# Attention of four head pairs as one list of items, SSM rows stored in two parts, and the last branch's rows loaded earlier

## The chip, the core and the metric

The kernel runs on one core of a Trainium2 chip. TensorE (PE in the profile; its weight loads are PEld) multiplies, VectorE (DVE), ScalarE (ACT) and GpSimd (POOL) work on tiles, and SyncE (SP) issues the transfers. The metric is the device time of one execution in microseconds (us).

## What is computed

One layer of a hybrid encoder, for a prompt of 1024 tokens and 32 sample tokens with a cache of 512 past positions, model width 1024, all in fp32. Cut to what matters here:

```python
z = einsum('btd,de->bte', h, w_in)                  # h: modulated RMSNorm of x
u, zs, q, k, v, za, qi, ki, wi, gm = split(z)
ys = gelu(ssm_scan(u, ...))                         # branch A, width 512
ys = ys * sigmoid(ys @ w_glu + b_glu) * silu(zs)
score = einsum('bth,bths->bts', wi, relu(qi . ki))  # indexer, 8 heads
idx = top_k(score, 256)                             # per query, among causal keys
ya = attend(q, k[idx], v[idx]) * silu(za)           # branch B, 8 heads of 64
merged = sigmoid(g_s) * (ys @ w_ps) + sigmoid(g_a) * (ya @ w_pa)
y = rms_norm(x + gate * (merged @ w_o), g_final)
```

Keys, values, indexer keys and the final SSM states are outputs too.

## The kernel before

Every fp32 product is three matmuls: an operand is split in a high part, rounded to TensorE's fp32r format, and a low part, the remainder, and `mm3` adds high x high, weight high x low and weight low x high (lines 245 to 247). `split` (L53) makes the parts: a cast (L55 on ScalarE, L57 on another engine) and a subtraction (L58). Activations are kept with channels on partitions and 1056 tokens (1024 and 32) on the free axis, in three column blocks of 352, chosen by `ns(n)`.

On TensorE, VectorE and ScalarE the order of the program is the order in which the code is written. GpSimd's and SyncE's instructions are placed by a scheduler. Each engine runs its queue in order.

**The filler stream.** The products with `w_in` that a later stage needs are jobs of the stream `Z` (class `Stream`, L551). A job (K1, V1, Q1, and m0 to m7) yields a step after each `mm3` of one column block and one k: 24 steps for a `w_in` job of 8 k, 12 for an m job of 4. `Z.run(us)` takes steps worth that time, at 0.483 us each, `Z.until(name)` takes all up to a job's end, `Z.upto(name)` allows jobs up to that one, and `Z.after(us, f)` calls `f` after that many us of steps. A step that isn't there (all allowed jobs are used up) ends `run` and drops its credit.

**The stages,** as they lie in the trace of before: GLU (266 to 304 us) ends in `ysD`, the SSM branch's rows in DRAM. The indexer's scores follow, then the selection (420 to 570): 31 iterations search each query's threshold bit by bit, ScalarE counting (L1549) and VectorE counting (L1551), and VectorE updating the keys (L1621, L1628, L1614). K, V and Q of pair 0 are made under it: their splits run on VectorE (casts) and GpSimd (subtractions, L58 and L1348). Marks of the selected keys follow.

**Attention** runs over four head pairs (p = 0 to 3; 632 to 900 us). `attend(p, ...)` (L1387) has a list of items: for each head e of the pair eight row blocks of 128 queries (`Rows`), and one `Sample` item for the sample tokens. An item has five parts: scores (L1363), maxima with the mask (L1369, VectorE), exponentials (L1376, ScalarE), normalization (L1383 or L1385), transposes with split (L1446, L1448, L1449) and the product with V (`out`, L1465 its low half). They are taken as a pipeline: in round k the scores of item k, the output of item k − 3, the transposes of item k − 2 and the exponentials of item k, with filler between them. `attend` runs three rounds more with no new item, and then the caller takes the rest of Q of the next pair (`Z.until`) and splits V of the next pair (`values`, L1347 and L1348). K of a head is read from its tile into a shifted one by DMA (`khead`, `kd`). In pairs 0 to 2 the filler is K, V and Q of the next pair; in pair 3 it is m0 to m7.

**The SSM branch's products** (`psjob`, m0 to m7, `ys @ w_ps`) need `ys` in parts: `ps_branch` loads 12 blocks of 128x352 in four transfers' worth of buffers at the start of pair 3 and splits them on ScalarE and VectorE, four rounds in a row (`extra`). The m jobs also load gate rows (`tgl`) into buffers that they share (`stg`).

**The last branch** (`branch`, `ya @ w_pa`) starts after m7: it loads pairs 0 to 2's rows of `ya` from `yaD` (L1725) through the two `stg` buffers, splits each (1056 columns, L55 and L58) and runs 8 jobs of 12 `mm3`. Pair 3's parts (`b3H`, `b3L`) are made by the attention itself. Then come the output product and the final norm (930 to 1073).

## Time and profile before

| | us |
|---|---|
| median of 3 runs | 1079.08 |
| lowest and highest | 1078.77, 1080.61 |
| the profiled execution | 1074.72 |
| its span | 1072.9 |
| busy in it: TensorE, VectorE, ScalarE, GpSimd | 1000.9, 765.6, 537.1, 246.9 |

The profiled execution is one run with its own time, 0.4% below the median of the others; 1.8 us of it lie outside the span. Times in the rows below count from the span's start. The mean granted TensorE clock over the span is 0.978 of full speed; the column PEclk of a stretch gives the clock there. An idle time in brackets behind an instruction is that of its engine just before it, and the arrow names what ended last there. Some matmul records can be missing, so counts of matmuls in a stretch are a few per cent rough.

### The profile page before, as it was taken

Reading aid. Unit: us, or ns where it says so; the run is one execution under the profiler, and the core shown is the slowest. Engines: PE = TensorE matmul, PEld = TensorE weight load, DVE = VectorE, ACT = ScalarE, POOL = GpSimd, SP = SyncE. Lnnn points to the kernel's source line nnn. Section 1 sums busy time; section 2 is a strip of 40 time slices with the busy share of each in tenths; the row PEclk is TensorE's granted clock in tenths of the full one; section 3 lists DMA queues with packets and bytes.
Section 4 is the critical chain, followed back from the end, with each engine's and each line's share of the span. In section 5 each row is a group of like instructions: output and inputs, shape, how many; then the busy total and the mean of one; then the engine's idle time right before and its main releaser. Section 6 shows DMA issues by size and latency. Waiting matters only on the chain.

```text
span 1072.9 us, 17009 instructions
## 1 busy us (share of the span) xinstructions
PE 1000.9 (93%) x6130; PEld 926.7 (86%) x6130; DVE 765.6 (71%) x1757; ACT 537.1 (50%) x1145; POOL 246.9 (23%) x465
## 2 busy tenths in 40 slices
...
GB/s 349 218 43 120 108 81 93 79 107 200 160 157 102 59 40 39 71 69 92 80 100 80 121 102 60 121 59 78 64 51 100 130 63 173 172 170 138 112 75 59
DMA packets 114321, 115.24 MB, mean 107 GB/s; under 512 B 13121, under 2 KB 90901, under 8 KB 114237
## 3 DMA queue, kind: packets, MB, share of 16 engines
...
HBM read 79.29 MB, written 30.08 MB: 102 GB/s over the span
## 4 chain that ended last, share of the span: by engine, by line
PE 51%; ACT 9%; DVE 8%; issue 4%; DMA 1%; POOL 0%; POOLq 0%; ACTq 0%; DVEq 0%
PE pz L245 7%; PE pz L247 6%; PE pz L246 6%; ACT junkb L1549 6%; PE pss L1363 3%; PE pt L1446 3%; PE psm L1874 3%; PE psm L1876 2%; PE psm L1875 2%; PE pss L247 2%; PE pss L245 2%; PE pss L246 2%; DVE junk L1551 2%; PE pspo L1465 2%; PE pspo L1463 2%
## 5 line engine op out<-in xcount | busy, mean ns | idle before, releaser
L245 PE MATMUL pz<-hH,wh 128*128 128x352 f32 (+1 forms) x824 | 280.1, 340 | 6.8 <-DVE zt L669 4.3
L246 PE MATMUL pz<-hL,wh 128*128 128x352 f32 (+1 forms) x824 | 269.1, 327 | 0.8 <-DVE hL L58 0.2
L247 PE MATMUL pz<-hH,wl 128*128 128x352 f32 (+1 forms) x824 | 268.4, 326 | 0.0
L238 POOL TENSOR_TENSOR wl<-raw,wh 128x256 fp32r<-128x256 f32 (+1 forms) x184 | 130.5, 736 | 169.9 <-ACT wh L233 155.6
L245 PEld LDWEIGHTS pz<-hH,wh 128*128 128x128 f32 (+1 forms) x824 | 155.9, 189 | 11.8 <-DVE zt L669 4.9
L246 PEld LDWEIGHTS pz<-hL,wh 128*128 128x128 f32 (+1 forms) x824 | 156.0, 189 | 4.1 <-DVE hL L58 2.0
L247 PEld LDWEIGHTS pz<-hH,wl 128*128 128x128 f32 (+1 forms) x824 | 155.7, 189 | 0.4
L1549 ACT ACTIVATE junkb<-sco,thr 128x896 bf16<-128x896 f32 (+3 forms) x128 | 103.6, 809 | 27.9 <-DVE thr L1628 20.0
L1551 DVE TENSOR_SCALAR_CACHE_REDUCE junk<-sco,thr 128x1024 bf16<-128x1024 f32 (+2 forms) x96 | 96.9, 1010 | 2.3
L245 PE MATMUL pss<-hH,wh 128*128 128x352 f32 x256 | 84.5, 330 | 7.8 <-ACT tg L680 5.2
L247 PE MATMUL pss<-hH,wl 128*128 128x352 f32 x256 | 84.1, 328 | 1.2 <-POOL wl L238 1.2
L246 PE MATMUL pss<-hL,wh 128*128 128x352 f32 x256 | 83.8, 327 | 0.0
L237 POOL CAST wh<-raw 128x256 fp32r<-128x256 f32 x88 | 34.8, 434 | 166.5 <-PE pz L246 143.2
L1376 ACT ACTIVATE Sm<-Sm,mx 128x128 f32<-128x128 f32 (+8 forms) x68 | 52.6, 774 | 13.5 <-DVE mx L1369 13.4
L1449 DVE TENSOR_TENSOR PL<-pt,PH 128x512 fp32r<-128x512 f32 (+2 forms) x96 | 50.6, 552 | 11.3 <-ACT PH L1448 10.1
L245 PEld LDWEIGHTS pss<-hH,wh 128*128 128x128 f32 x256 | 49.1, 192 | 10.4 <-POOL wh L237 5.2
L1448 ACT CAST PH<-pt 128x512 fp32r<-128x512 f32 (+2 forms) x96 | 43.2, 481 | 27.4 <-PE pt L1446 24.8
L1207 DVE SCALAR_TENSOR_TENSOR sco<-rl,wi,sco 128x384 f32<-128x384 f32 (+6 forms) x49 | 47.3, 977 | 11.7 <-ACT rl L1202 10.1
L1202 ACT ACTIVATE rl<-pss 128x384 f32<-128x384 f32 (+6 forms) x56 | 40.9, 738 | 28.3 <-PE pss L1200 20.3
L233 ACT CAST wh<-raw 128x1024 fp32r<-128x1024 f32 (+2 forms) x43 | 36.1, 839 | 32.7 <-PE pz L246 21.0
L1876 PE MATMUL psm<-o,mL 128*128 128x512 f32 (+1 forms) x136 | 51.7, 382 | 0.0
L1875 PE MATMUL psm<-o,mH 128*128 128x512 f32 (+1 forms) x136 | 51.6, 381 | 0.0
...
## 6 DMA issues: line engine op xcount, KB each, us to landing
...
```

Source lines behind the costliest of these rows:

```text
L238: leng.tensor_sub(wl[:, c], raw[:, c], f32(wh[:, c]))
L245: te.matmul(ps, wh, xh, start=first, stop=False)
L246: te.matmul(ps, wh, xl, start=False, stop=False)
L247: te.matmul(ps, wl, xh, start=False, stop=last)
L1207: ve.scalar_tensor_tensor(sco[i][:m, :nk], rl[:m, :nk], w, sco[i][:m, :nk], op0=ALU.mult, op1=ALU.add)
L1376: se.activation(P, P, AF.Exp, scale=-1.0, bias=self.mx, accum_out=self.rs)
L1448: se.copy(PH[:, b0:b1_, oc], src)
L1449: ve.tensor_sub(PL[:, b0:b1_, oc], src, f32(PH[:, b0:b1_, oc]))
L1549: se.activation(junkb[:m, :nk], x[:m], AF.Sign, bias=t, accum_out=cnt[:m, k:k + 1])
L1551: ve.tensor_scalar(junk[:m, :nk], x[:m], t, None, op0=ALU.is_lt, op1=ALU.add, accum_out=cnt[:m, k:k + 1])
L1875: te.matmul(ps, mh, wl, start=False, stop=False)
L1876: te.matmul(ps, ml, wh, start=False, stop=last)
```

## The change

- **One list.** `attention(p, X)` only returns a pair's items. One loop runs over the items of all four pairs, so the last outputs of one pair stand in the rounds of the next pair's first scores. Filler is set per pair and head (`FA`, us per item, with `FF` per row block): 2.0 and 1.3 in pairs 0 and 1, 2.4 and 1.6 in pair 2, 1.5 in pair 3, where it was 1 (1.4 in pair 3). Q of the next pair is allowed from head 1 on. V is a tile per head; head 0's is split three rounds ahead of the pair's end, head 1's after the last output.
- **K** goes to DRAM once (`kd`) and is read back from there per head. The subtractions of pair 0's K and V run on VectorE (`heng_v`).
- **SSM rows in two parts.** GLU casts and subtracts its result per block of 352 columns on ScalarE and GpSimd and stores both parts (24 transfers of 128x352 instead of 4 of 128x1056). When Q3 ends, `switch` issues 24 direct loads of those parts, into the place of the activations' low part; no split is left. The m jobs start behind them, still under pair 2.
- **The last branch's rows** are loaded right after the last attention item, before the rest of m0 to m7, into buffers of their own (the place of the transposed scores and of the output weights), and split at 4, 5 and 6 us of the steps that follow.
- **Stream.** Where no step is available, `run` advances the delayed calls (`tick`).

```diff
@@ -35,7 +35,7 @@
-FA = ((1, 0.08), (1, 0.08), (1, 0.08), (1.4, 0.08))
+FA, FF, SW, SA, SB = ((2.0, 1.3), (2.0, 1.3), (2.4, 1.6), (1.5, 1.5)), 0.08, 1.2, 4.0, 1.0
@@ -616,19 +616,21 @@
...
-                for t in self.later:
-                    t[0] -= 1
-                for t in [t for t in self.later if t[0] <= 0]:
-                    self.later.remove(t)
-                    t[1]()
+                self.tick()
                 return True
+
+        def tick(self):
+            for t in self.later:
+                t[0] -= 1
+            for t in [t for t in self.later if t[0] <= 0]:
+                self.later.remove(t)
+                t[1]()
         def run(self, us):
             self.credit += us / self.STEP
             while self.credit >= 1:
                 if not self.step():
-                    self.credit = 0.0
-                    return
+                    self.tick()
                 self.credit -= 1
...
@@ -1061,7 +1063,7 @@
...
-    ysD = [dram.tile([128, NT], F32, name=f"ysD{q}") for q in range(4)]
+    ysD = [[dram.tile([128, NT], F32, name=f"ys{h}D{q}") for q in range(4)] for h in "HL"]
...
@@ -1093,8 +1095,10 @@
...
             ve.scalar_tensor_tensor(z2[:, c], th, 1.0, z2[:, c], op0=ALU.add, op1=ALU.mult)
-        sp.dma_start(ysD[q], z2)
...
+            yo = [gp.tile([128, G3], F32R, name=f"yo{h}", bufs=3) for h in range(2)]
+            split(yo[0], yo[1], z2[:, c], se, ge)
+            for h in range(2):
+                sp.dma_start(ysD[h][q][:, c], f32(yo[h]))
...
@@ -1254,10 +1258,10 @@
...
             for hf_ in range(2):
-                sp.dma_start(kd[64 * hf_:64 * hf_ + 64], X.kf[64 * e:64 * e + 64, c])
+                sp.dma_start(kd[64 * hf_:64 * hf_ + 64], X.kd[64 * e:64 * e + 64, c])
             def parts():
-                split(kH[:, c], kL[:, c], kd, ve, ge)
+                split(kH[:, c], kL[:, c], kd, ve, leng)
...
@@ -1309,6 +1313,9 @@
...
         def kside(self):
+            self.kd = dram.tile([128, T], F32, name=f"kd{self.p}")
+            sp.dma_start(self.kd, self.kf[:, 0:T])
+
...
@@ -1338,16 +1346,16 @@
...
-                khead(self, self.want.pop(0), KA, done)
-
-        def values(self):
-            V2 = self.V2 = ap_.tile([128, 8, 2, 128], F32R, name="V2", bufs=1)
-            for e in range(2):
-                vsrc = self.vt[:, 0:8, 64 * e:64 * e + 64]
-                ve.tensor_copy(V2[:, :, e, 0:64], vsrc)
-                ge.tensor_sub(V2[:, :, e, 64:128], vsrc, f32(V2[:, :, e, 0:64]))
-            self.cvt = ap_.tile([128, 4, 128], F32, name="cvt", bufs=1)
-            sp.dma_start(self.cvt, cv[:, :, self.cs])
+                khead(self, self.want.pop(0), self.heng_v, KA, done)
+
+        def values(self, e):
+            V = self.V2[e] = ap_.tile([128, 8, 128], F32R, name=f"V{e}", bufs=1)
+            vsrc = self.vt[:, 0:8, 64 * e:64 * e + 64]
+            ve.tensor_copy(V[:, :, 0:64], vsrc)
+            self.heng_v.tensor_sub(V[:, :, 64:128], vsrc, f32(V[:, :, 0:64]))
+            if e:
+                self.cvt = ap_.tile([128, 4, 128], F32, name="cvt", bufs=1)
+                sp.dma_start(self.cvt, cv[:, :, self.cs])
...
@@ -1384,22 +1392,32 @@
...
-    def attend(p, X, fills, half, last_s, extra=None):
-        kall, V2, vts, cvt = X.kall, X.V2, X.vts, X.cvt
-        qsm = X.qsm.rearrange("p e q -> p (e q)")
-        ya = at2.tile([128, NT], F32, name="ya", bufs=1)
+    def attention(p, X):
+
+        Y = {}
+
+        def begin():
+            if p < 3:
+                Y[0] = stg.tile([128, NT], F32, name="ya", tag="stg")
+                sp.dma_start(Y[0], zaD[p])
+            else:
+                Y[0] = f32(ap_.tile([128, T], F32R, name="qs1", bufs=2))
+                Y[1] = at2.tile([128, TS], F32, name="ys", bufs=1)
+                sp.dma_start(Y[0], zaD[p][:, 0:T])
+                sp.dma_start(Y[1], zaD[p][:, T:NT])
+
...
@@ -1480,39 +1498,7 @@
...
-        fa_, fb_ = fills
-        q = []
-        for k, it in enumerate(items + [None] * 3):
-            f = fa_ + fb_ * (it.i + 1 if it else 5)
-            if it:
...
-        if p < 3:
-            sp.dma_start(yaD[p], ya)
+        return items, begin, lambda: sp.dma_start(yaD[p], Y[0])
...
@@ -1556,7 +1542,8 @@
-        Z.after(1.0, X.values)
+        Z.after(1.0, lambda: X.values(0))
+        Z.after(2.0, lambda: X.values(1))
@@ -1565,31 +1552,16 @@
...
     def ps_branch():
-        bH, bL = ({(q, n): fb.tile([128, G3], F32R, name=f"b{h}{q}{n}") for q in range(4) for n in range(3)}
-                  for h in range(2))
-        src = {}
-
...
-        PB.extend((bH, bL))
-        for t in range(3):
-            load(t)
-        for b, c in ((0, 4), (4, 6), (6, 9), (9, 12)):
-            for k in range(b, c):
-                n, q = divmod(k, 4)
-                split(bH[q, n], bL[q, n], src[k // 3][:, ns(k % 3)], se, ve)
-            if b == 0:
-                load(3)
-            yield
+        for h in range(2):
+            PB.append({(q, n): late["fb"].tile([128, G3], F32R, name=f"b{h}{q}{n}") for q in range(4) for n in range(3)})
+        for n in range(3):
+            for q in range(4):
+                for h in range(2):
+                    sp.dma_start(f32(PB[h][q, n]), ysD[h][q][:, ns(n)])
...
     at2 = stT.enter_context(tc.tile_pool(name="at2", bufs=1, side="right", reuse_waits="tile"))
+    seq, first, half, end = [], {}, {}, {}
     for p in range(4):
-        if p < 3:
-            nxt = HD[p + 1]
...
-            attend(p, X, FA[p], half, last_s)
...
-            nxt.values()
-            X = nxt
-    st.close()
-    b3H, b3L = (zfp.tile([128, NT], F32R, name=n, tag="zf", bufs=2) for n in ("b3H", "b3L"))
-    fin = ctx.enter_context(tc.tile_pool(name="fin", bufs=1, reuse_waits="tile"))
+        items, begin, store = attention(p, HD[p])
+        first[len(seq)] = (p, begin)
+        half[len(seq) + [k for k in range(1, len(items)) if items[k].e == 1 != items[k - 1].e][0]] = p
...
+    at = lambda k: seq[k] if 0 <= k < len(seq) else None
+    late = {}
+
+    def switch():
+        st.close()
+        late["fin"] = ctx.enter_context(tc.tile_pool(name="fin", bufs=1, reuse_waits="tile"))
+        late["fb"] = stB.enter_context(tc.tile_pool(name="fb", bufs=1, reuse_waits="tile"))
+        ps_branch()
+        Z.after(SW, lambda: Z.upto("m7"))
+    HD[3].qjob.end = switch
     stB = ExitStack()
-    fb = stB.enter_context(tc.tile_pool(name="fb", bufs=1, reuse_waits="tile"))
-    pb = ps_branch()
...
-    attend(3, X, FA[3], None, lambda: None, extra)
+    for k in range(len(seq) + 3):
+        it = at(k)
+        if k in first:
+            p, begin = first[k]
+            k0 = k
+            if p:
+                Z.until(f"Q{p}")
+            if p == 3:
+                b3H, b3L = (zfp.tile([128, NT], F32R, name=n, tag="zf", bufs=2) for n in ("b3H", "b3L"))
+            else:
+                Z.upto(f"V{p + 1}")
+            begin()
+        if it:
+            e_ = max(it.e, 0) if it.e >= 0 or p == 3 else 1
+        f = FA[p][e_] + FF * (it.i + 1 if it else 5)
+        if it:
+            it.scores()
+        if k in half and p < 3:
+            HD[p + 1].want.append(0)
+            HD[p + 1].heads()
+            Z.upto(f"Q{p + 1}")
+        if p and k == k0 + 2:
+            HD[p].want.append(1)
+            HD[p].heads()
+        if it:
+            it.maxima()
+        if at(k - 1):
+            at(k - 1).norm(0)
+        run(f * 0.4)
+        if at(k - 3):
+            at(k - 3).out()
+        if k - 3 in end and end[k - 3][0] < 3:
+            end[k - 3][1]()
+            HD[p].values(1)
+        if k + 3 in end and p < 3:
+            Z.until(f"v{p + 1}")
+            HD[p + 1].values(0)
+        run(f * 0.3)
+        if at(k - 2):
+            at(k - 2).turn()
+        if at(k - 1):
+            at(k - 1).norm(1)
+        if it:
+            it.exps()
+        run(f * 0.3)
+
+    stT.close()
...
+    aH, aL = [], []
+    for q in range(3):
+        src = f32(wo.tile([128, 2, 512], F32R, name="src", tag=("o16", "o17", "o07")[q]).rearrange("p a b -> p (a b)"))
+        sms = wo.tile([128, TS], F32, name=f"srs{q}")
+        sp.dma_start(src, yaD[q][:, 0:T])
+        sp.dma_start(sms, yaD[q][:, T:NT])
+        h_, l_ = (mp.tile([128, NT], F32R, name=f"b{h}{q}", tag="b" + "0123"[2 * q + h] if q < 2 else f"b{4 + h}")
+                  for h in range(2))
+        aH.append(h_)
+        aL.append(l_)
+
+        def parts(h_=h_, l_=l_, src=src, sms=sms):
+            split(h_[:, 0:T], l_[:, 0:T], src, se, ve)
+            split(h_[:, T:NT], l_[:, T:NT], sms, se, ve)
+        Z.after(SA + q * SB, parts)
+    aH.append(b3H)
+    aL.append(b3L)
     Z.until("m7")
     Z.flush()
     dv_.close()
     pe_.close()
...
-    branch(mp, yaD, I["w_pa"].rearrange("o d e -> (o d) e"), 1, evac_a, lambda: ps_x("m", 4))
+    w_pa = I["w_pa"].rearrange("o d e -> (o d) e")
+    for f in range(8):
+        wh, wl = wsplit(w_pa[:, 128 * f:128 * f + 128], 4, 128)
+        tg = stg.tile([128, NT], F32, name="tgl", tag="stg")
+        sp.dma_start(tg, thD[8 + f])
+        for n in range(3):
+            ps = ps_x("m", 4)
+            for k in range(4):
+                mm3(ps[:, :G3], wh[:, k], wl[:, k], aH[k][:, ns(n)], aL[k][:, ns(n)], k == 0, k == 3)
+            evac_a(f, ns(n), tg[:, ns(n)], ps[:, :G3])
...
```

The order on VectorE in the selection, where pair 0's V and K are split between two iterations. Before (`sco` are scores, `thr` the thresholds, `kd` is K as loaded, `tm` is V by token):

```order
L1551 TENSOR_SCALAR junk,cnt<-sco_3116,thr 128x1024
L1551 TENSOR_SCALAR junk,cnt<-sco_3114,thr 128x768
L1551 TENSOR_SCALAR junk,cnt<-sco_3112,thr 128x512
L1347 CAST V_4646<-tm 128x8x64 x2
L57 CAST kH_4622<-kd 128x512
L1621 TENSOR_TENSOR keep<-cnt,lim 128x7
L1628 SCALAR_TENSOR_TENSOR thr<-keep,nxt 128x7
```

The same place after:

```order
L1537 TENSOR_SCALAR junk,cnt<-sco_3188,thr 128x1024
L1537 TENSOR_SCALAR junk,cnt<-sco_3186,thr 128x768
L1537 TENSOR_SCALAR junk,cnt<-sco_3184,thr 128x512
L1354 CAST V_4729<-tm 128x8x64
L1355 TENSOR_TENSOR V_4729<-tm,V_4729 128x8x64
L57 CAST kH_4696<-kd 128x512
L58 TENSOR_TENSOR kL_4697<-kd,kH_4696 128x512
L1593 TENSOR_TENSOR keep<-cnt,lim 128x7
```

The two subtractions, which were GpSimd's, now stand in VectorE's queue ahead of the key update; one head's V is split here and the other's one iteration earlier.

The order on TensorE where pair 3 begins. Before (`hH`, `hL` are the parts of the layer's input in a `w_in` job, here the end of Q3; `b` are the SSM rows of m0):

```order
L245 MATMUL pz<-hH_82,wh 128x352
L246 MATMUL pz<-hL_85,wh 128x352
L247 MATMUL pz<-hH_82,wl 128x352
L1363 MATMUL pss<-kH_8459,qs_8577 128x512
L1363 MATMUL pss<-kL_8460,qs_8577 128x512
L1363 MATMUL pss<-kH_8459,qs_8577 128x384
...
L1363 MATMUL pss<-kH_8459,qs_8577 128x128
L1363 MATMUL pss<-kL_8460,qs_8577 128x128
L245 MATMUL pz<-b_8822,wh 128x352
L246 MATMUL pz<-b_8834,wh 128x352
L247 MATMUL pz<-b_8822,wl 128x352
```

After, from the end of Q3 on (which is now in the middle of pair 2's head 1; `kall` are the sample item's keys):

```order
L245 MATMUL pz<-hH_82,wh 128x352
L246 MATMUL pz<-hL_85,wh 128x352
L247 MATMUL pz<-hH_82,wl 128x352
L1464 MATMUL pt<-idf,Sm 128x128 x5
L1371 MATMUL pss<-kH_8053,qs_7619 128x512
...
L1464 MATMUL pt<-idf,Sm 128x128 x6
L245 MATMUL pz<-b_8770,wh 128x352
L246 MATMUL pz<-b_8782,wh 128x352
L247 MATMUL pz<-b_8770,wl 128x352
L1371 MATMUL pss<-kall,qsm 64x512
L1371 MATMUL pss<-kall,qsm 64x32
L245 MATMUL pz<-b_8773,wh 128x352
```

The six score products in a row are gone; the first steps of m0 stand between transposes, scores and outputs of pair 2.

The order of SyncE's transfers at the end of the attention. Before (`tgl` are gate rows, `raw` weights, `src` rows of `ya`, `xo` the layer's input for the final addition):

```order
L1840 DMA xo<-in_x_prompt 128x1024 x2
L1594 DMA tgl<-thD_210 128x1056
L224 DMA raw<-in_w_pa 128x4x128
L1725 DMA src<-yaD_4102 128x1056
L224 DMA raw<-in_w_pa 128x4x128
L1725 DMA src<-yaD_4103 128x1056
L1725 DMA src<-yaD_4104 128x1056
```

After:

```order
L1566 DMA tgl<-thD_210 128x1056
L224 DMA raw<-in_w_pa 128x4x128
L1836 DMA xo<-in_x_prompt 128x1024 x2
L1722 DMA src<-yaD_4174 128x1024
L1723 DMA srs_9864<-yaD_4174 128x32
L1722 DMA src<-yaD_4175 128x1024
L1723 DMA srs_9870<-yaD_4175 128x32
L1722 DMA src<-yaD_4176 128x1024
```

The rows of `ya` no longer wait for buffers that the last m jobs hold; the two loads of `xo`, which were ahead of the last gate rows, stand right before them.

## Rows read from the trace of the kernel before

**Rows 1.** Page, part 1: busy us, share of the span, instructions.

```profile
PE 1000.9 (93%) x6130; PEld 926.7 (86%) x6130; DVE 765.6 (71%) x1757; ACT 537.1 (50%) x1145; POOL 246.9 (23%) x465
```

**Rows 2.** Table by stretch: start:end, us, busy (count) by engine, PEclk, DMA share, GB/s.

```profile
280.00:304.00 24.00, 24.00 (x153) 23.72 (x152) 12.96 (x20) 7.78 (x15) 0.00 (x0) 1.00 0.48 158
457.80:501.00 43.20, 39.84 (x231) 39.32 (x230) 39.63 (x83) 32.13 (x73) 20.57 (x30) 0.92 0.33 91
632.00:820.00 188.00, 181.50 (x1235) 170.35 (x1234) 124.44 (x353) 112.57 (x263) 58.50 (x122) 1.00 0.25 68
820.00:850.00 30.00, 22.75 (x129) 20.20 (x128) 20.33 (x57) 15.99 (x34) 6.04 (x9) 0.94 0.40 122
850.00:900.00 50.00, 48.27 (x326) 45.18 (x326) 37.86 (x110) 28.87 (x70) 14.16 (x34) 1.00 0.27 80
900.00:930.00 30.00, 24.68 (x140) 23.52 (x139) 10.89 (x18) 6.32 (x9) 5.20 (x12) 0.94 0.70 233
```

**Rows 3.** Timeline of PE, pairs 0 to 2: start, us, instruction, [idle before <-releaser].

```profile
640.79 0.98 PE L1446 MATMUL pt<-idf,Sm 128*128 128x128 f32 x7 [0.62 <-ACT Sm L1383]
...
691.17 0.33 PE L1446 MATMUL pt<-idf,Sm 128*128 128x128 f32 x1 [1.66 <-DVE Sm L1385]
...
711.63 1.09 PE L1446 MATMUL pt<-idf,Sm 128*128 128x128 f32 x8 [0.62 <-ACT Sm L1383]
...
761.93 0.33 PE L1446 MATMUL pt<-idf,Sm 128*128 128x128 f32 x1 [1.67 <-DVE Sm L1385]
```

**Rows 4.** Timeline of PE, start of pair 3.

```profile
834.64 0.33 PE L1363 MATMUL pss<-kH,qs 128*128 128x128 f32 x1 [3.28 <-DVE mx L1369]
```

**Rows 5.** Timelines of ACT and DVE, start of pair 3: splits of the SSM rows.

```profile
831.64 1.62 ACT L55 CAST b<-src 128x352 fp32r<-128x352 f32 x4
...
832.14 1.83 DVE L58 TENSOR_TENSOR b<-src,b 128x352 fp32r<-128x352 f32 x4 [1.58 <-ACT b L55]
```

**Rows 6.** Table by stretch: low clock, and transfers at pair 3's start.

```profile
834.50:838.00 3.50, 3.36 (x16) 3.29 (x16) 2.43 (x8) 2.48 (x5) 0.00 (x0) 0.58 0.55 170
923.60:927.00 3.40, 3.31 (x12) 3.31 (x13) 1.30 (x2) 0.15 (x1) 0.00 (x0) 0.53 0.61 184
832.00:834.00 2.00, 0.00 (x0) 0.00 (x0) 1.86 (x5) 1.27 (x4) 0.00 (x0) 1.00 0.71 205
834.00:836.00 2.00, 1.36 (x6) 1.36 (x7) 1.82 (x6) 0.48 (x1) 0.00 (x0) 0.77 0.84 257
```

**Rows 7.** Timelines of SP (issues), ACT and PE, start of the last branch.

```profile
910.75 0.33 SPq L1725 DMA_DIRECT2D src<-yaD  x1
...
916.88 0.80 SPq L1725 DMA_DIRECT2D src<-yaD  x2
...
914.49 1.07 ACT L55 CAST b<-src 128x1056 fp32r<-128x1056 f32 x1 [3.69 <-DMA src<-yaD]
...
922.40 0.91 PE L245 MATMUL psm<-b,wh 128*128 128x352 f32 x4 [3.77 <-ACT b L55]
```

**Rows 8.** Timelines of DVE and POOL in the selection, and one subtraction in GLU.

```profile
457.61 0.17 DVE L1621 TENSOR_TENSOR keep<-cnt,lim 128x7 int32<-128x7 f32 x1
...
464.11 0.17 DVE L1621 TENSOR_TENSOR keep<-cnt,lim 128x7 int32<-128x7 f32 x1
...
467.73 0.77 DVE L1347 CAST V<-tm 128x512 fp32r<-128x512 f32 x2
...
480.44 1.29 POOL L58 TENSOR_TENSOR kL<-kd,kH 128x512 fp32r<-128x512 f32 x1 [2.44 <-DVE kH L57]
...
480.46 1.29 DVE L1621 TENSOR_TENSOR keep<-cnt,lim 128x7 int32<-128x7 f32 x1
...
496.60 0.17 DVE L1621 TENSOR_TENSOR keep<-cnt,lim 128x7 int32<-128x7 f32 x1
...
500.80 0.17 DVE L1621 TENSOR_TENSOR keep<-cnt,lim 128x7 int32<-128x7 f32 x1 [0.59 <-ACT junkb L1549]
...
285.04 0.69 DVE L238 TENSOR_TENSOR wl<-raw,wh 128x512 fp32r<-128x512 f32 x1 [1.29 <-ACT wh L233]
```

115 lines of the change are left out of this document (20 added, 95 removed).

## The prediction

> **What bounds the kernel now.** I read the busy shares first. TensorE is busy for 93% of the span and no other engine for more than 71% [rows 1], so only two things shorten this kernel: stretches in which TensorE idles (or runs at the lower clock), and stages in which another engine sets the pace. The change moves work between engines and in time, but the number of TensorE instructions stays the same to within two. The table by stretch [rows 2] then says where there is something to win in the stages the change touches. In pairs 0 to 2 of the attention (632 to 820 us) TensorE idles 188 − 181.5 = 6.5 us; at the start of pair 3 (820 to 850) 7.25; under the SSM branch's products (850 to 900) 1.7; at the start of the last branch (900 to 930) 5.3. The selection (457.8 to 501) has idle time too, but there the loop of VectorE and ScalarE sets the end. GLU (280 to 304) has none: TensorE is busy for 24.0 of 24. Last I read what ends the idle times [rows 3, 4, 7] and the granted clock behind them [rows 6].
>
> **The change part by part.** Each term is the gain against the profiled execution's own 1074.72 us.
>
> (a) Pairs 0 to 2. The idle time is few long waits at turns between pairs and heads: two of 0.62 us for ScalarE, 1.66 and 1.67 for VectorE [rows 3], and one more of 0.53. They arise because a pair's pipeline of three items drains, the rest of Q's steps is put behind it in one piece, and the next pair begins with nothing beside it. With one list of items the next pair's scores stand under the last pair's transposes, and more filler goes to each item. What is left: V's subtraction now falls inside a pair, and Q's evacuation (two subtractions on VectorE per 352 columns) falls among head 1's maxima, the wait that ends last there. The five sum to 5.1, which is the upper bound. I take 3.0, nearer to it, since the two big waits are the turns that vanish; the lower bound is 1.
>
> (b) Start of pair 3. Here 7.25 us of idle time stand [rows 2], 3.28 of them in one wait behind VectorE's maxima [rows 4]. VectorE was late because it and ScalarE were splitting the SSM rows (12 casts of 0.405 and 12 subtractions of 0.46 [rows 5]). After it the clock is at 0.58 for 3.5 us [rows 6], between 1.2 and 2.4 GHz, after a stretch in which TensorE had idled; that costs (1 − 0.58) × 3.5 = 1.5 more. Together 8.7. The change removes the splits here and the drain, and puts in 24 direct loads of 176 KB, each pair of which one m0 step waits for. Do they come in time? By the order, TensorE reaches the steps that need loads 8, 16 and 24 some 39, 62 and 102 matmuls after Q3's end. At 48.27 / 326 = 0.148 us each [rows 2] that is 5.8, 9.2 and 15.1 us. For the supply I take 257 GB/s, the best window of the old loads at this place [rows 6], and 1.6 us ahead of it (the row load issued at 910.75 was used at 914.49 [rows 7]; 0.541 MB at 257 GB/s is 2.1 of these 3.7). Each group of 8 is 1.44 MB, so they land at 7.2, 12.8 and 18.4: TensorE is at most 3.6 us late. At 205 GB/s, the other window [rows 6], it is 7.6. Queued on SP behind the 24 loads are pair 3's K, the weights of m3, m1's gate rows (VectorE's evacuations wait for those) and pair 2's store, which nothing needs before (d); I put 0.9 on them, a quarter of the row load's 3.7. So 8.7 − 3.6 − 0.9 = 4.2, with bounds 0 and 8: what the loads cost is the largest unknown of the sum.
>
> (c) 850 to 900 us: 1.7 idle [rows 2], spread thin. With the splits' remainder gone and filler at 1.5 per item I take 0.7 (0 to 1.7).
>
> (d) Last branch. Before, the first row load is issued at 910.75, when TensorE is nearly out of SSM products; the cast waits 3.69 us for it, and TensorE 3.77 us for a later row's cast [rows 7]. With the idle 5.3 [rows 2] goes the clock at 0.53 for 3.4 us [rows 6], 1.6 more: 6.9 in all. After, the loads are issued once the last attention item is through, with 16 product steps still to run. A step is 3 matmuls of 24.00 / 153 = 0.157 us [rows 2], so they cover 7.5 us, and the third row's low part is needed 26 matmuls later, at 11.6. But in SP's queue two input loads (1.05 MB) stand right ahead, free to go some 2.4 us before the last output product. Setup 1.6 plus 2.67 MB at 257 GB/s is 12.0, so the third row lands at 9.6. A cast of 1.07 us [rows 7] and a subtraction of about 1.4 (0.69 for 512 columns [rows 8], times two) end near 11.9; at 205 GB/s, 14.5. I leave 1.4 us of wait, the middle of 0.3 and 2.9 with some weight on the first: gain 5.5 (2 to 6.9).
>
> (e) Selection. Pair 0's V and K splits lie in its eight iterations between the key updates at 457.61 and 500.80. A free iteration lasts 4.20 (496.60 to 500.80), but these eight took 43.2 [rows 8]. The reason is in one pair of rows: GpSimd's subtraction starts at 480.44 and takes 1.29 us, VectorE's update of 128x7 starts at 480.46 and also takes 1.29, where it normally takes 0.17 [rows 8]. The small updates on the path of the keys wait out GpSimd's instruction. The change does these six subtractions on VectorE, in order, 0.69 each (the row at 285.04 [rows 8]); a cast is 0.39 (two in 0.77). An iteration also has 0.59 us in which VectorE waits for ScalarE's counts [rows 8], which absorbs that much. So: the first, with Q's evacuation (6.5 now, to 464.11), plus V's cast and subtraction gives 7.6; the second has V, kH and kL, 4.2 + 2.2 − 0.6 = 5.8; three with kH and kL, 4.7 each; three free ones, 4.2. Sum 40.1, gain 3.1 (0, if subtractions beside GpSimd's weight splits stretch too, to 4.5).
>
> (f) GLU. It gains 12 casts on ScalarE (4.9 us at 0.405), 12 subtractions on GpSimd (0.88 each: 1.29 [rows 8] × 352/512) and 20 more stores, in a stage where GpSimd is idle, ScalarE busy 7.8 of 24 and VectorE 13.0 [rows 2]. TensorE has no gap, so these must stay behind it: the unit of 12 matmuls is 1.9 us, and ScalarE's work per unit is with the cast about 2.0. I take −0.5 (−2.4, if half of the casts show, to 0).
> What the rows show of GpSimd beside VectorE is the stretch in (e). The Trainium skill ("SBUF — State Buffer", section "Who interferes with whom") says that the two share a port pair held for a whole instruction, and that a VectorE instruction with two inputs in SBUF meets a GpSimd one that reads SBUF. By it VectorE's gating product in GLU could stand behind the new subtractions: −1.0 rather than −0.5, and the total 15.5.
>
> K's reading back through DRAM costs nothing as long as the 5 us of filler between load and split hide it; uncovered, a load (1.6 us plus 0.26 MB at 257 GB/s) would hold VectorE's queue, the next maxima behind it, for at most 2.6 us. The four matmuls on the modulation weights that come earlier, I cost at nothing: they are the same four.
>
> Sum: 3.0 + 4.2 + 0.7 + 5.5 + 3.1 − 0.5 = 16.0, giving 1058.7 on the profiled execution's own time. The median of the runs is 1079.08, 0.4% above that execution; taken from the median, the forecast is **1063.1 us**. The lower bounds sum to 0.6, the upper to 26.2.
>
> **The rivals.**
> *The waits move to VectorE.* Filler per item rises and Q's evacuation and V's splits now lie among maxima and subtractions; VectorE is at 66% in pairs 0 to 2 and at 76% from 850 to 900 [rows 2]. Then (a) to (c) give 2 of their 7.9 and the time is 1069. For it: the longest waits of before end on VectorE [rows 3, 4]. Against: 63 us of VectorE's time are free in pairs 0 to 2.
> *The last branch's rows are late all the same*, so that the change doesn't do there what it says: the two input loads ahead and the product steps' own gate rows take the queue, (d) gives 1.0, and the time is 1067.6. For it: the DMA share is 0.70 there already [rows 2].
> *Slower: the 24 loads.* One mechanism: each m0 step stands in TensorE's program between attention items, so a late load stops the attention too, and behind the loads SP holds pair 3's K and m1's gate rows. 4.33 MB must land; the sum is used up when TensorE is 19.6 us late, so when the last load lands 34.7 us after Q3's end: below 4.33 / 33.1 = 131 GB/s. At 100 GB/s it would be 29.8 late and the time 1089. For it: the whole stretch around ran at 122 GB/s [rows 2]. Against: that was not a limit, two windows inside it show 205 and 257 [rows 6].
> The Trainium skill ("DMA: Bandwidth & Descriptors", section "Bandwidth") speaks against this part of the change: transfers should be of 1 MiB or more, and it gives 138 GB/s for one of 64 KB. At that figure, an estimate, the loads would take 33 us and the time would be 1077.
> *Near no change*: several terms at their lower ends, 1078.
>
> **How the numbers follow.** Forecast 0.58 (its own range 1056 to 1069), waits on VectorE 0.15, late last branch 0.11, near no change 0.06, slower through the loads 0.10. A measurement of this kernel tells about 0.2% from no change, 2.2 us. Faster by more: 0.58 + 0.15 + 0.11 = 0.84; within: 0.06; slower by more: 0.10. The range, 1055 to 1076, takes in the forecast's bounds but for their far ends and both rivals on the fast side; outside are slower, no change and a little below 1055.
>
> **What would show it.** (a) In pairs 0 to 2 no wait of TensorE over 1 us at the turns. (b) The SSM products of m0 begin between the last items of pair 2, TensorE's waits there are on DMA and sum to under 5 us, and the granted clock stays at 1.0. (d) The first product of the last branch starts within 1.5 us of the last SSM product. (e) Eight iterations of the selection in about 40 us, the small updates at 0.17. (f) TensorE still busy for 24 of 24 in GLU. The prediction is wrong if m0's steps wait for loads by more than 8 us, if maxima of head 1 become the longest waits, or if the selection does not shorten: then VectorE's subtractions are stretched by GpSimd as well.

## The result, and the profile after

The changed kernel takes 1065.74 us (median of 4 runs, 1062.95 to 1069.62) beside 1079.32 before (1078.77 to 1080.61): a ratio of 0.9875, 95% interval 0.9843 to 0.9907, or 13.6 us less. Forecast were 1063.1 in a range of 1055 to 1076, and 16.0 us less. The way it came about is another matter: the terms at pair 3 and at the last branch came out near, those for pairs 0 to 2, for the selection and for GLU did not, and 2.5 us came from an edit that had been costed at nothing.

The profiled execution of the changed kernel took 1065.50 us, span 1063.7, only 9.2 less than the profiled one of before. This difference misleads. I cut each trace at the same matmuls: the first product of GLU, the first gate product behind the indexer's scores, the first key update of the selection, the last gate product, and the last product of the last branch. Ahead of GLU every engine has the same instructions in the same order in all kernels of this study, and yet GLU begins at 278.6 us in the trace of before and between 280.1 and 286.3 in the others, of either kind. So the trace of before was an early one, 4.6 us faster than its own median, and stages are compared behind that point. All times in this table are differences of starts of matmuls (of VectorE's updates for the first update and the eight iterations; the last column runs to the end of the last matmul) on the timelines:

| kernel | GLU begins | GLU | first gate product to first update | eight iterations | attention, SSM products, last branch | GLU's begin to end |
|---|---|---|---|---|---|---|
| before | 278.6 | 22.8 | 7.8 | 43.2 | 356.3 | 787.3 |
| after | 284.1 | 24.2 | 5.3 | 42.3 | 343.8 | 772.6 |
| e1_rraw_late | 286.3 | 24.3 | 7.7 | 42.7 | 343.7 | 776.2 |
| e2_pool_subs | 281.4 | 24.2 | 5.3 | 43.8 | 344.3 | 774.9 |
| e3_glu_dve | 281.4 | 23.2 | 5.3 | 42.7 | 343.7 | 773.6 |
| e4_m_lag0 | 281.8 | 24.2 | 5.3 | 42.7 | 340.5 | 771.3 |
| e5_rows_late | 280.9 | 24.3 | 5.3 | 43.0 | 351.4 | 784.7 |
| e6_filler_old | 282.8 | 24.3 | 5.3 | 43.0 | 344.2 | 777.4 |
| e7_direct_loads | 285.4 | 24.3 | 7.8 | 43.4 | 350.6 | 786.0 |
| e8_rows_early | 280.2 | 22.8 | 7.7 | 43.2 | 353.7 | 788.9 |
| e9_parts_no_list | 284.6 | 24.3 | 7.7 | 43.3 | 346.5 | 779.1 |
| e10_glu_dve_m_lag0 | 282.4 | 23.0 | 5.3 | 43.0 | 340.5 | 769.8 |
| e11_loads_twice | 281.1 | 24.2 | 5.3 | 42.7 | 354.7 | 786.1 |
| e12_shares | 280.1 | 23.1 | 5.3 | 42.7 | 338.7 | 768.7 |

The last column also holds the rest of the selection, which differs by up to 4.6 us between traces of the same order; the stage columns repeat within 0.1 to 0.7 us. From GLU's begin on, the change is worth 14.7 us in the two traces: 12.5 in attention with the last branch, 2.5 ahead of the first update, 0.9 in the eight iterations and −1.4 in GLU.

The page and the table by stretch of the changed kernel, to be read beside [rows 1] and [rows 2] (columns as there):

```profile
PE 1001.7 (94%) x6130; PEld 927.4 (87%) x6130; DVE 761.8 (72%) x1754; ACT 538.4 (51%) x1148; POOL 252.6 (24%) x471
```

```profile
284.00:308.00 24.00, 23.39 (x144) 22.51 (x143) 12.23 (x16) 12.34 (x24) 8.46 (x9) 1.00 0.70 217
462.80:505.10 42.30, 39.97 (x239) 39.45 (x239) 38.13 (x89) 31.92 (x73) 13.95 (x24) 0.96 0.33 100
616.50:820.00 203.50, 197.43 (x1322) 186.14 (x1321) 130.08 (x370) 114.11 (x270) 66.74 (x134) 1.00 0.30 91
820.00:850.00 30.00, 28.26 (x189) 25.46 (x188) 23.70 (x67) 18.36 (x37) 5.52 (x14) 1.00 0.69 222
850.00:900.00 50.00, 47.64 (x323) 44.30 (x322) 36.22 (x105) 28.98 (x68) 12.88 (x32) 1.00 0.24 71
900.00:914.00 14.00, 12.57 (x79) 11.97 (x78) 6.92 (x15) 5.54 (x12) 3.40 (x8) 1.00 0.79 283
914.00:930.00 16.00, 16.00 (x101) 16.00 (x100) 14.07 (x27) 6.03 (x12) 8.30 (x16) 1.00 0.74 232
```

TensorE's work is the same. The holes at the start of pair 3 (7.25 us idle in 30 before) and of the last branch (5.3) are gone, and with them the stretches at a low clock [rows 6]: the granted clock is 1.00 in all stretches from 616 on. GLU, which had no gap, has one now. What ends the idle times is new as well. TensorE's timeline, four of the waits (start, duration, instruction, idle before and releaser):

```profile
644.17 0.66 PE L1241 MATMUL pt<-idf,zf 128*128 128x128 f32 x4 [0.92 <-DVE PL L1467]
...
683.74 0.97 PE L1483 MATMUL pspo<-PL,V 128*128 128x256 f32 x6 [0.61 <-DVE PL L1467]
...
720.85 0.66 PE L1328 MATMUL pt<-idf,ckt 128*128 128x128 f32 x4 [0.70 <-DVE PL L1467]
...
907.92 0.43 PE L245 MATMUL pz<-b,wh 128*128 128x352 f32 x1 [1.36 <-DVE m L1569]
```

In pairs 0 to 2 the long waits at the turns [rows 3] have vanished, but eight of 0.2 to 0.92 us for the transposes' low part (PL) sum to 4.8; all idle time there is 6.1 us by the table (203.50 − 197.43), where it was 6.5. From Q3's end to the last branch 4.0 of 5.5 us end with an evacuation of an SSM product (m) on VectorE.

### The profile page after: what moved, and what is told of

Read it like the earlier page. It is cut to its first block, busy times and chain, and to the rows that moved or that the text cites. A ratio compares the mean times of both kernels' runs of the same rounds, so it can differ in the third digit from the quotient of the medians.

```text
span 1063.7 us, 17065 instructions
## 1 busy us (share of the span) xinstructions
PE 1001.7 (94%) x6130; PEld 927.4 (87%) x6130; DVE 761.8 (72%) x1754; ACT 538.4 (51%) x1148; POOL 252.6 (24%) x471
## 4 chain that ended last, share of the span: by engine, by line
PE 48%; DVE 9%; ACT 8%; issue 5%; POOL 1%; POOLq 0%; ACTq 0%; DVEq 0%
PE pz L245 7%; PE pz L246 6%; PE pz L247 6%; ACT junkb L1535 5%; PE pss L1371 3%; DVE junk L1537 3%; PE psm L1870 3%; PE psm L1872 3%; PE psm L1871 3%; PE pt L1464 2%; PE pspo L1483 2%; PE psm L245 1%; PE psm L247 1%; PE psm L246 1%; PE pspo L1481 1%
## 5 line engine op out<-in xcount | busy, mean ns | idle before, releaser
L1467 DVE TENSOR_TENSOR PL<-pt,PH 128x512 fp32r<-128x512 f32 (+2 forms) x96 | 50.4, 552 | 24.3 <-ACT PH L1466 23.3
L1871 PE MATMUL psm<-o,mH 128*128 128x512 f32 (+1 forms) x136 | 51.5, 380 | 0.0
L1870 PE MATMUL psm<-o,mH 128*128 128x512 f32 (+1 forms) x136 | 51.3, 380 | 0.0
```

Of the source, the lines that this page charges most:

```text
L1467: ve.tensor_sub(PL[:, b0:b1_, oc], src, f32(PH[:, b0:b1_, oc]))
L1870: te.matmul(ps, mh, wh, start=first, stop=False)
L1871: te.matmul(ps, mh, wl, start=False, stop=False)
```

## The experiments

**e1_rraw_late.** Only the place of the last four modulation matmuls, and of VectorE's operations on them, is put back.

```diff
-        Z.after(RM, mm)
+        Z.after(RM if i < 3 else 1000.0, mm)
```

> The changed kernel with one thing put back: the last four matmuls on the modulation weights (pg from rraw), and with them VectorE's five operations on their result, again stand behind the last score products. In the trace of the changed kernel the time from the first gate product after the scores (first pss from hH) to the first key update of the selection is 5.3 us, before the change it was 7.8. Theory: these five operations (3.2 us on VectorE) are the cause, so here it is 7.8 again and the whole 2.5 us come back. Rival: the difference comes from where the scores end, and it stays near 5.3. Everything else as in the changed kernel: GLU 24.5 us, eight iterations with pair 0's splits 42.3, attention 297, last branch 46.5.

7.7 us: the theory. The run took 1071.31 us (1078.15 before beside it). VectorE's timeline shows what stands ahead of the first count:

```profile
419.13 0.68 DVE L1134 TENSOR_TENSOR grow<-pg,grow 2x512 f32<-2x512 f32 x1
...
420.53 2.13 DVE L1134 TENSOR_TENSOR grow<-pg,grow 2x512 f32<-2x512 f32 x3
422.69 0.41 DVE L1135 TENSOR_SCALAR grow<-grow 2x512 f32<-2x512 f32 x1
```

Four additions of 0.7 us and a scaling of 0.4 for two rows of 512 elements. In the changed kernel they lie among the score products (401 to 407 us), and the stretch from GLU's last product to the first gate product is not longer for it (108.7 us, 108.8 before).

**e2_pool_subs.** Pair 0's subtractions go back to GpSimd.

```diff
-            self.eng, self.V2, self.heng_v = eng, [None, None], ve if p == 0 else ge
+            self.eng, self.V2, self.heng_v = eng, [None, None], ge
```

> The changed kernel with pair 0's subtractions of V and K back on GpSimd. The prediction put 3.1 us on this move; the traces show the eight iterations at 43.2 us before and 42.3 after. Theory A (the move gains little, because VectorE's own subtractions and updates are stretched by GpSimd's weight splits as well): the eight iterations take 43 to 43.5 us, 1 more than in the changed kernel, with key updates (128x7) of 1.2 to 1.3 us beside GpSimd's subtractions. Theory B (the prediction's): 45 us or more. Theory C: no gain at all, below 42.5.

43.8 us: nearest to theory A, 0.3 above its figures. The eight iterations take 43.2 to 43.4 in the four traces with before's order, 42.3 to 43.0 in the nine others with VectorE's subtractions; the move is worth 0.2 to 1.6 us (0.8 to 1.5 by e2 alone). The whole run took 1065.10 us. The blocked update is back (VectorE, then GpSimd):

```profile
472.58 1.26 DVE L1593 TENSOR_TENSOR keep<-cnt,lim 128x7 int32<-128x7 f32 x1
...
472.41 1.41 POOL L1355 TENSOR_TENSOR V<-tm,V 128x512 fp32r<-128x512 f32 x1 [1.04 <-DVE V L1354]
```

**e3_glu_dve.** GLU's subtractions move from GpSimd to VectorE.

```diff
-            split(yo[0], yo[1], z2[:, c], se, ge)
+            split(yo[0], yo[1], z2[:, c], se, ve)
```

> The changed kernel with GLU's 12 new subtractions on VectorE instead of GpSimd. In the changed kernel GLU (first to last product) takes 24.5 us against 23.1 before, and VectorE's products z from th and z take 0.91 to 1.25 us where a GpSimd subtraction runs beside them, 0.52 elsewhere. Theory: the two engines stand in each other's way, and that is what costs 1.4 us; without GpSimd's work all z products are back at 0.52 and GLU takes 23.1 to 23.6 us, though VectorE has 12 x 0.46 = 5.5 us more to do. Rival: ScalarE's 12 casts are the cost; then GLU stays at 24.5 or is longer. The next stage's first product should not be later than it is now.

23.2 us instead of 24.2: the theory, though VectorE has 12 operations more. The run took 1063.78 us. First a product and a GpSimd subtraction of the changed kernel, then a subtraction and a product of e3:

```profile
292.80 0.92 DVE L1097 SCALAR_TENSOR_TENSOR z<-th,z 128x352 f32<-128x352 f32 x1 [1.01 <-ACT th L1096]
...
292.39 0.95 POOL L58 TENSOR_TENSOR yo<-z,yo 128x352 fp32r<-128x352 f32 x1 [1.58 <-ACT yo L55]
```

```profile
291.06 0.53 DVE L58 TENSOR_TENSOR yo<-z,yo 128x352 fp32r<-128x352 f32 x1 [0.55 <-ACT yo L55]
...
291.81 0.53 DVE L1097 SCALAR_TENSOR_TENSOR z<-th,z 128x352 f32<-128x352 f32 x1 [0.22 <-ACT th L1096]
```

VectorE's product starts at 292.80, inside GpSimd's subtraction (292.39 to 293.34), and ends 0.38 us behind it: it seems to do most of its own work only when the other is through. Alone it takes 0.53. 0.4 us of GLU's extra time remain; ScalarE's casts, VectorE's additional subtractions and the stores are what e3 leaves, and they were not tried apart.

**e4_m_lag0.** The SSM products are evacuated right behind the product.

```diff
-                        if self.lag:
+                        if self.lag and b.name[0] != "m":
```

> The changed kernel with the evacuations of the SSM products (m jobs) written right behind their products instead of two steps later. In the changed kernel 4.0 of the 5.5 us that TensorE idles from the end of Q3 to the last branch end with such an evacuation on VectorE (0.44, 0.92, 1.28 and 1.36 us). Theory: they wait in VectorE's queue behind attention's own operations, which wait for ScalarE; earlier in the queue they are done in time, these four waits go, and the stretch is 3 to 4 us shorter. Rival 1: the gate rows' loads are late, and the waits stay. Rival 2: VectorE now waits for TensorE at the evacuations and makes attention's maxima late: other waits take their place, no gain.

The four waits are gone, 340.5 us instead of 343.8, the whole run 1061.84. The waits of TensorE from 819 to 909 us, by releaser (sum, number, longest):

```profile
PE pt L1464 <- ACT Sm L1391: 1.6, 3, 0.8
PE pspo L1483 <- DVE PL L1467: 0.6, 1, 0.6
```

So the evacuations were late because of their place in VectorE's queue, not because of the gate rows.

**e5_rows_late.** The changed kernel, with the last branch's rows loaded as before: the block stands behind `Z.until("m7")` again, ahead of `w_pa`.

```diff
-        sp.dma_start(src, yaD[q][:, 0:T])
-        sp.dma_start(sms, yaD[q][:, T:NT])
+        src = stg.tile([128, NT], F32, name="src", tag="stg")
+        sp.dma_start(src, yaD[q])
...
-        Z.after(SA + q * SB, parts)
+        split(h_, l_, src, se, ve)
```

> The changed kernel with the last branch's rows loaded and split as before the change: through the two shared buffers, behind the last SSM product job. From the first to the last product of the last branch the traces show 53.2 us before and 46.2 in the changed kernel. Theory (the prediction's term for the last branch, there 5.5 us): the late loads cost it all, so 51.5 to 53.5 us here, with a wait of 3 us or more for a cast behind a DMA and the clock near 0.5 behind it, and the attention stage stays at 297.6. Rival: part of the 7 us comes from the attention's end (fewer operations of VectorE in the way); then it is below 50.

The last branch takes 53.2 us, the attention 298.3, together 351.4: the theory, 7.7 us more than the changed kernel. The run took 1074.51 us. ScalarE and TensorE at the last branch, and its table by stretch:

```profile
921.51 1.07 ACT L55 CAST b<-src 128x1056 fp32r<-128x1056 f32 x1 [5.70 <-DMA src<-yaD]
...
922.64 1.54 PE L245 MATMUL psm<-b,wh 128*128 128x352 f32 x4 [4.45 <-ACT b L55]
```

```profile
922.00:926.00 4.00, 3.36 (x11) 3.16 (x12) 2.52 (x2) 1.66 (x2) 0.00 (x0) 0.57 0.30 96
```

**e6_filler_old.** The one list with the old filler values.

```diff
-((2.0, 1.3), (2.0, 1.3), (2.4, 1.6), (1.5, 1.5))
+((1.0, 1.0), (1.0, 1.0), (1.0, 1.0), (1.4, 1.4))
```

> The changed kernel with the filler per item as it was before the change (1.0, 1.0, 1.0 and 1.4 us, the same for both heads) in the one list. From the last gate product to the first product of the last branch (attention with the SSM products) the traces show 303.1 us before and 297.6 after. Theory: the list alone removes the waits at the turns (two of 1.66 and the pair-3 ones), and the filler values decide how long TensorE waits for the splits of the transposes: with less filler these waits (0.6 to 0.9 each, eight of them in pairs 0 to 2) get longer and more numerous, and the steps left over stand in one piece at each pair's end: 299 to 302 us. Rival: the filler values don't matter, 297 to 298.

With the last branch 344.2 us, 0.4 more than with the new values (its boundary to the last branch can't be used alone, since some of the last products are interleaved there): the rival. The waits are at other places, though. Up to Q3's end TensorE now idles only 2.9 us, with two waits for PL instead of eight (table by stretch; the changed kernel has 197.43 busy in a stretch of the same length). What is won there is lost behind it, with 2.84 us for Q's evacuation at pair 3's start, 1.37 for an m evacuation and 1.31 for the row casts (TensorE's rows):

```profile
619.50:823.00 203.50, 200.64 (x1358) 191.01 (x1356) 131.10 (x389) 119.92 (x283) 65.37 (x135) 1.00 0.31 94
```

```profile
825.99 0.79 PE L1371 MATMUL pss<-kH,qs 128*128 128x512 f32 x1 [2.84 <-DVE qs L1305]
...
911.57 0.40 PE L245 MATMUL pz<-b,wh 128*128 128x352 f32 x1 [1.31 <-ACT b L55]
```

The run took 1069.08 us.

**e7_direct_loads.** The kernel before, with the SSM rows in two parts and the direct loads alone.

```diff
-        sp.dma_start(ysD[q], z2)
+            split(yo[0], yo[1], z2[:, c], se, ge)
+            for h in range(2):
+                sp.dma_start(ysD[h][q][:, c], f32(yo[h]))
...
-    pb = ps_branch()
+    ps_branch()
```

> The kernel before with one part of the change: GLU stores the SSM rows in two parts, and 24 direct loads at the start of pair 3 take the place of 12 splits; the attention stays in four separate pairs. Theory: the splits on ScalarE and VectorE made the maxima at pair 3's start late (3.28, 1.46 and 0.89 us of waits and 1.5 for the clock); with them gone the attention stage falls from 303.1 to 298 to 300 us, and what is left are waits for the loads, which can start only at Q3's end. Rival 1: the drain of the pipeline is the cause, and the stage stays above 301.5. Rival 2: the 24 loads are too slow there (no filler of pair 2 ahead of them), with waits of m0's products on DMA of 5 us and more, above 303. GLU takes 1.2 to 1.5 us longer than 22.8, as in the changed kernel.

The attention stage takes 296.9 us, better than expected and no longer than in the changed kernel; with the last branch 350.6. Of the three waits at pair 3's start (1.46, 0.89 and the 3.28 of [rows 4]) two are left, and m0's first product waits for nothing:

```profile
838.48 0.50 PE L1365 MATMUL pss<-kH,qs 128*128 128x512 f32 x1 [1.46 <-DVE qs L1303]
...
840.91 0.79 PE L1365 MATMUL pss<-kH,qs 128*128 128x512 f32 x1 [0.90 <-DVE mx L1371]
...
843.10 0.60 PE L245 MATMUL pz<-b,wh 128*128 128x352 f32 x1
```

The 3.28 us wait was the splits'. The run took 1080.13 us all the same (1078.58 before beside it), with GLU's begin at 285.4 and 1.5 us lost in GLU: a part that is worth 5.6 us in its stage can't be seen in one run's time.

**e8_rows_early.** The kernel before, with the last branch's early rows alone: the changed kernel's block from `aH, aL = [], []` to `Z.after(..., parts)`, behind `attend(3, ...)`.

```diff
     attend(3, X, FA[3], None, lambda: None, extra)
+    stT.close()
+    mbp.close()
...
+        sp.dma_start(src, yaD[q][:, 0:T])
...
+        Z.after(4.0 + q * 1.0, parts)
     Z.until("m7")
```

> The kernel before with one part of the change: the last branch's rows loaded right behind the last attention item into buffers of their own and split 4, 5 and 6 us later. Here 34 SSM product steps (16 us) are left at that point, not 16 steps. Theory: the last branch takes 46 to 47 us instead of 53.2, no first product of it waits, and the attention stage stays at 303: 6 to 7 us in all. Rival: the loads take the place of the SSM jobs' gate rows in the queue and the attention stage grows by 1 us or more.

353.7 us: 2.6 gained, not 6 to 7. Neither theory: the first row isn't there when its split is called. ScalarE's cast waits 4.88 us for it, VectorE's subtraction 4.26 for the cast, and the evacuations of the 34 steps that are left stand behind it in VectorE's queue, so that TensorE waits 2.60 us for one of them (ScalarE, TensorE, then VectorE; the clock is 0.58 from 914 to 918):

```profile
911.71 1.05 ACT L55 CAST b<-src 128x1024 fp32r<-128x1024 f32 x1 [4.88 <-DMA src<-yaD]
...
914.87 0.66 PE L245 MATMUL pz<-b,wh 128*128 128x352 f32 x1 [2.60 <-DVE m L1597]
...
912.79 1.23 DVE L58 TENSOR_TENSOR b<-src,b 128x1024 fp32r<-128x1024 f32 x1 [4.26 <-ACT b L55]
...
914.30 0.51 DVE L1597 SCALAR_TENSOR_TENSOR m<-tgl,pz 128x352 f32<-128x352 f32 x1
```

The run took 1078.15 us.

**e9_parts_no_list.** e7 and e8 together on the kernel before: the one list, its filler and K through DRAM are left out.

```diff
-    pb = ps_branch()
+    ps_branch()
...
     attend(3, X, FA[3], None, lambda: None, extra)
+    stT.close()
...
+        Z.after(4.0 + q * 1.0, parts)
```

> The kernel before with two parts of the change: the SSM rows stored in two parts with 24 direct loads, and the last branch's rows loaded early into buffers of their own. The attention stays in four separate pairs with the old filler. From the last gate product to the last product of the last branch (attention, SSM products and last branch) the traces show 356.3 us before, 343.8 in the changed kernel, 350.6 with the direct loads alone and 353.7 with the early rows alone. Theory A (the one list is worth nothing by itself; the waits at the turns were replaced by as many behind VectorE): 343 to 345 us here. Theory B (the prediction's, 3 us for the list in pairs 0 to 2): 346 to 348. If the early rows are worth here only the 2.6 us that they brought alone, 348.

346.5 us: the list, with its filler and K's way, is worth 2.7, within theory B's figures. But not where the prediction had it. In pairs 0 to 2 this kernel idles 6.6 us and the changed one 6.1. The rest is at the end, where the changed kernel has only 16 product steps left behind the attention and this one 34, with e8's wait again:

```profile
909.57 0.43 PE L245 MATMUL pz<-b,wh 128*128 128x352 f32 x1 [2.24 <-DVE m L1584]
```

The run took 1072.82 us.

**e10_glu_dve_m_lag0.** The edits of e3 and e4 together.

```diff
-            split(yo[0], yo[1], z2[:, c], se, ge)
+            split(yo[0], yo[1], z2[:, c], se, ve)
...
-                        if self.lag:
+                        if self.lag and b.name[0] != "m":
```

> The changed kernel with two things of the runs before together: GLU's new subtractions on VectorE (GLU 23.2 instead of 24.2 us) and the SSM products' evacuations right behind their products (attention with last branch 340.5 instead of 343.8). If the two add up, 4.3 us less than the changed kernel: 1061 to 1062 us beside 1079 before, ratio 0.983 to 0.985. If the earlier selection or scores give something back, up to 1064.

1062.18 us (median of 5, 1060.98 to 1065.78) beside 1079.66, ratio 0.9839 (0.9812 to 0.9867). Both gains stand in the table (23.0 and 340.5). Against the changed kernel's 0.9875 the intervals overlap; that it is faster rests on the stages.

**e11_loads_twice.** The price of late loads.

```diff
+        for _ in range(2):
             for n in range(3):
                 for q in range(4):
                     for h in range(2):
                         sp.dma_start(f32(PB[h][q, n]), ysD[h][q][:, ns(n)])
```

> The changed kernel with each of the 24 loads of the SSM rows issued twice (all 24, then all 24 again into the same places; the products wait for the second). In the changed kernel SP issues one load each 0.47 us, no product waits for one, and a load is issued some 6.5 us ahead of the step that uses it. Theory (the rival of the prediction in which late loads stop the attention): 24 x 0.47 = 11.3 us later, so m0's steps wait 6 to 10 us on DMA in all, the attention's items behind them too, and the stage grows by as much, from 297.6 to 304 to 309 us. If more than 24 loads in a row also run slower each, or the gate rows behind them come late, more than 309. If the list has enough to do meanwhile, below 302.

The attention stage takes 308.5 us, 10.9 more, the whole run 1075.97. One wait, at m0's first product, and the low clock behind it:

```profile
832.32 0.66 PE L245 MATMUL pz<-b,wh 128*128 128x352 f32 x1 [9.79 <-DMA b<-ysHD]
```

```profile
832.00:836.00 4.00, 3.68 (x8) 1.78 (x9) 0.27 (x1) 0.00 (x0) 0.00 (x0) 0.55 1.07 379
```

The wait is not made up anywhere, and 1 us more is lost behind it, where the clock is 0.55: the prediction's slower rival has its mechanism and price, but not its condition. How far the changed kernel was from it can be estimated. The load that this product waits for is issued 4.0 us ahead of it (SyncE):

```profile
828.28 0.43 SPq L1561 DMA_DIRECT2D b<-ysHD  x1
```

In the changed kernel the tightest of the 24, the 16th, is issued 7.1 us ahead of its product (824.44 and 831.50), so its loads were some 3 us ahead.

**e12_shares.** e10, with a round's filler divided otherwise.

```diff
-        run(f * 0.4)
+        run(f * 0.45)
...
-        run(f * 0.3)
+        run(f * 0.1)
...
-        run(f * 0.3)
+        run(f * 0.45)
```

> The kernel of e10 (GLU's subtractions on VectorE, SSM evacuations right behind their products) with the filler of a round divided otherwise: 45% ahead of an item's output, 10% ahead of the transposes and 45% behind them, where it was 40, 30 and 30. In pairs 0 to 2 of the changed kernel TensorE idles 5.5 us, 4.8 of them in eight waits of 0.43 to 0.92 us for the low part of the transposed scores on VectorE (PL), which the product with V and the next transposes need. Theory: they are a matter of how much filler lies between an item's transposes and its output (70% of a round then, 90% here); the waits fall below 2 us and attention with last branch from 340.5 to 336 to 338 us. Rival: with only 10% of filler ahead of the transposes these wait for the normalization (Sm on ScalarE or VectorE) instead, and the stage stays above 340.

338.7 us, between theory and rival. The waits for PL in pairs 0 to 2 fall from 4.7 to 2.4 us, 1.0 of waits for the normalization remains, and the SSM loads, needed earlier, are late for the first time (waits of TensorE, 613 to 820 us):

```profile
PE pt L1241 <- DVE PL L1467: 1.8, 2, 0.9
PE pt L1464 <- ACT Sm L1391: 1.0, 3, 0.6
PE pz L245 <- DMA b<-ysHD: 0.6, 1, 0.6
PE pz L246 <- DMA b<-ysLD: 0.6, 1, 0.6
PE pt L1328 <- DVE PL L1467: 0.4, 2, 0.2
PE pspo L1483 <- DVE PL L1467: 0.2, 1, 0.2
```

1059.19 us (median of 5, 1057.63 to 1061.47) beside 1079.79: ratio 0.9814, 0.9795 to 0.9834, below the whole interval of the changed kernel (0.9843 to 0.9907). Against e10 (0.9812 to 0.9867) the intervals overlap; that it is faster than e10 rests on the stage, 338.7 us instead of 340.5.

## Why the prediction was right, and where its steps were not

The time lies 2.6 us above the forecast and in its range. That the total is so near is in part luck: (a), (e) and (f) together gave 5.7 us less than forecast, the modulation matmuls and the other terms 4.6 more. By terms, forecast and measured:

| term | forecast | measured, in the two traces |
|---|---|---|
| (a) pairs 0 to 2 | 3.0 | 0.4 (idle 6.5 to 6.1) |
| (b) and (c) pair 3 | 4.9 | 5.5 (idle and clock 11.0 to 5.5) |
| (d) last branch | 5.5 | 7.0 |
| (e) eight iterations | 3.1 | 0.9 |
| modulation matmuls | 0 | 2.5 |
| (f) GLU | −0.5 | −1.4 |

(a) and (b) with (c) give 5.9 by idle time and clock; the stage itself shortened by 5.5 (303.1 to 297.6), and the 0.4 between them was not traced.

**(a)** failed at "the two big waits are the turns that vanish". They vanish, and eight smaller ones on VectorE take their place: it is the first rival, in this term alone, and the gain lies below the lower bound of 1. The raised filler has a part in it: with the old values the same list idles 2.9 us there (e6), a gain of 3.6, and loses it again from pair 3's start on, so that in the sum the filler's amount doesn't matter (0.4 us); e12 shows that its place in the round does. I had read what ended the old waits and not what would end last when they are gone: the transposes' low part, which stands in the same loop in every round.

**(b)** had the right size with a wrong step. The prediction counted the supply of all 24 loads from Q3's end on, and that is wrong. SyncE's issues in the changed kernel, the first, the sixth and the last of the 24, and m0's first product on TensorE:

```profile
811.34 0.36 SPq L1560 DMA_DIRECT2D b<-ysHD  x1
...
819.81 0.32 SPq L1560 DMA_DIRECT2D b<-ysLD  x1
...
828.54 0.32 SPq L1560 DMA_DIRECT2D b<-ysLD  x1
...
822.73 0.41 PE L245 MATMUL pz<-b,wh 128*128 128x352 f32 x1
```

Five loads find free memory 5 to 8.5 us ahead of Q3's end (819.9), and no product waits. The 3.6 us put down for that don't arise; what does arise are the m evacuations (4.0), which the prediction didn't have. The two errors cancel. e7 settles the cause: with the splits gone the stage takes 296.9 us even in separate pairs.

**(d)** The mechanism held and the leftover of 1.4 us was wrong: the first product of the last branch follows the last SSM product at once, and 325 to 395 GB/s moved from 906 to 918 us, not 257 (TensorE, then two stretches of the changed kernel):

```profile
913.62 0.32 PE L247 MATMUL pz<-b,wl 128*128 128x352 f32 x1
913.78 0.64 PE L245 MATMUL psm<-b,wh 128*128 128x352 f32 x3
```

```profile
906.00:910.00 4.00, 2.64 (x17) 2.35 (x16) 1.64 (x3) 1.23 (x2) 1.70 (x4) 1.00 1.00 386
910.00:914.00 4.00, 4.00 (x27) 4.00 (x26) 2.00 (x4) 2.33 (x4) 0.00 (x0) 1.00 1.03 395
```

e5 gives 7.7 for this part on top of the rest, e8 2.6 and e9 4.2 (350.6 to 346.5) where the attention leaves 34 steps behind it. So the gain depends on what stands behind the rows' splits. In the changed kernel the first row's cast waits too, 4.19 us, but with 16 steps left no product of TensorE waits behind it. That the number of steps is the cause was not tried by itself: in e6 28 are left, TensorE waits 1.31 us for a row's cast, and the total is only 0.4 us longer.

**(e)** failed in the sum, at "0.69 each" for the subtractions. In the changed kernel that holds for the two kL subtractions that meet no GpSimd instruction. The two others took 1.1 beside GpSimd's weight splits, and the three operations of one update 0.69, 0.65 and 0.66 instead of 0.17. The iterations with the two slow subtractions came out 0.4 us longer each than the forecast's, the one with that update 1.0; that is 1.8 of the missing 2.2 (VectorE, then GpSimd):

```profile
484.95 1.11 DVE L58 TENSOR_TENSOR kL<-kd,kH 128x512 fp32r<-128x512 f32 x1
...
495.70 0.69 DVE L1593 TENSOR_TENSOR keep<-cnt,lim 128x7 int32<-128x7 f32 x1
...
482.50 3.01 POOL L238 TENSOR_TENSOR wl<-raw,wh 128x256 fp32r<-128x256 f32 x4
...
494.34 3.42 POOL L238 TENSOR_TENSOR wl<-raw,wh 128x256 fp32r<-128x256 f32 x4
```

The lower bound had named this ("if subtractions beside GpSimd's weight splits stretch too"); the value should have been taken nearer to it, since those splits stand in the same rows of GpSimd's queue. What made up for it, 2.5 us, came from an edit that the prediction had costed at nothing, "they are the same four": the four matmuls are, but VectorE's five operations on them moved as well, from the head of the selection into the scores (e1).

**(f)** The step failed at "in a stage where GpSimd is idle". The stage's cost is not GpSimd's time but VectorE's, which it stops: four of the 12 products took 0.91 to 1.25 us instead of 0.52. Nor do the rows give "about 2.0" for ScalarE's work per unit: 7.78 us in 24 [rows 2] are 0.6 per unit of 1.9, 1.0 with the cast, so by the rows that reason for −0.5 falls away. The estimate from the Trainium skill ("SBUF — State Buffer", section "Who interferes with whom") in the prediction, −1.0, was nearer than mine, and e3 bears the rule out: without GpSimd's reads the products are back at 0.51 to 0.53 and 1.0 of the 1.4 us is gone.

The rivals: the first held in (a) and, with the m evacuations, took 4 us of (b) and (c); the second, late rows, did not happen; the third is priced by e11 and was some 3 us away from beginning, by the estimate there. The other transfer that was added, K through DRAM, shows no wait of its own in the stages; it was not tried alone.

What stays open: why GLU begins anywhere from 278.6 to 286.3 us with the same code ahead of it. A part is a wait of TensorE for VectorE's `zt` shortly before, which is either 1.55 to 1.58 or 3.10 to 3.11 us in the traces of either kind. Its cause was not looked for. The traces do show that the granted clock goes with GLU's begin: from the span's start to GLU it is 0.96 in the trace of before, the earliest, and 0.93 in e1's, the latest. (1 − clock) times that stretch is about 10 and 19 us, and GLU's begin less this amount lies between 266.4 and 270.4 us in all 14 traces. That this is the cause, and why the clock differs, is not shown.
